# A looser hand-written order for the expert stages of a one-core decoder step

## The chip, the cores and the metric

The program runs on one core of one Trainium2 chip. The metric is the device time of one launch in microseconds (us). A core has five engines, each with its own instruction queue, worked off in order: TensorE (PE in the profile: matmuls; PEld: its weight loads), VectorE (DVE), ScalarE (ACT), GpSimd (POOL) and SyncE (SP). An instruction at the head of a queue that waits for another engine holds up everything behind it.

## The reference, cut to what matters

One layer is computed for 320 tokens (256 of a prompt, 64 of 8 decoding sequences) of width 2048: attention and a gated unit, then a layer of single-neuron experts (PEER), then a gated per-layer embedding. The change touches only the experts and what borders on them:

```python
s1 = einsum('thc,nc->thn', q[:, :, 0], k1)   # 8 heads, 128 keys
s2 = einsum('thc,nc->thn', q[:, :, 1], k2)
v1, i1 = top_k(s1, 16); v2, i2 = top_k(s2, 16)
sc, ci = top_k(v1[..., :, None] + v2[..., None, :], 16)
e = i1[ci // 16] * 128 + i2[ci % 16]         # 16 of 16384 experts per head
g = softmax(sc)
act = gelu(einsum('thkd,td->thk', u_tab[e], x))
out = einsum('thkd,thk->td', v_tab[e], g * act)
```

## The kernel before, in words

Everything is computed in fp32 accuracy with three matmuls: weights and inputs are split into a high and a low part. ACT writes the high part (`w_hi`), DVE the low part (`w_lo`), both from the weights as loaded (`w_raw`).

For 240 of the 320 tokens the experts are not gathered but computed densely: all 16384 expert rows are multiplied, and the gates of experts that were not chosen are zero. The work comes in 256 **units** of 1 MB of weights: 128 u-units (`u_tab`; 128 experts for 240 tokens, into PSUM tag "mm") and 128 v-units (`v_tab`, into tag "o"). A unit is 48 matmuls of 240 columns, a **half unit** 24. `order` lists them: 32 u-units (LEAD), then 16 **groups** of 8 v-units, with 6 or 7 u-units after each. Each PSUM tag has two buffers. The other 80 tokens (the samples and the first 16 of the prompt) are served by gathered rows: 160 row steps on DVE, spread over the groups.

Inside `manual_schedule` the order on PE, ACT and DVE is the order of the code. The functions are:

- `prepare(n, h)`: the load, `w_hi` (ACT) and `w_lo` (DVE) of half h of unit n, written two units ahead. `multiply(n, h, q)`: 12 matmuls of it (a quarter of the unit). `finish(n)`: the GELU of a u-unit (ACT, into `act`), or the addition of a v-unit to `hT` (DVE).
- Routing: `choose` picks the 16 best keys (DVE), `soften` does the softmax, `key_tables` transposes the picks on PE. A budget sets how many steps stand in each half unit: 1.5 of a cost noted at each `yield`.
- Gate map: 30 **jobs**. `one_hots(j)` makes two tables on DVE (`e`, `p`; two buffers each), `map_products(j)` 16 matmuls on PE and two copies on ACT (`g_st`, two buffers); every second job POOL writes a megabyte to `gd` in DRAM. The jobs are spread evenly over the u-units from the end of the routing to unit U1 = 29.
- `fetch_g(g)`: a transfer issued from ACT's queue that brings the gates of group g back. The first one waits for the last write to `gd`.
- `rows_of`: 16 copies on ACT (`xd`) and 16 transposes on PE, each right behind its copy, for `xc` (in units 29 to 31) and for `xx` (in group 0).
- `weights(g)`: for each of a group's 8 activations a multiplication by the gates (DVE), the high part (ACT) and the low part (DVE). One is taken per half unit, the high part in the same half unit as its multiplication. Those of group 0 stand in one block before group 0.
- `add_samples`: 32 + 16 small matmuls and three additions, all after the second v-unit of the last group.

Half of a group's eight pairs of buffers (`tails`) are columns of the tiles `a` and `c` that the dense part doesn't use; the others are four pairs of tiles `wh`, `wl`. After the groups come `emb` (the embedding product), the split of `hT` into `a` and `c`, a sum of squares, and 16 units of the last gate. That part is in the order of the scheduler.

Of the kernel before, what the change touches and what calls it, by code (L numbers as in the profile page):

```python
# [52 lines left out]
def _build(ctx, tc, nc, a):  # L53
# [554 lines left out]
    def soften(i):  # L608

        g = R[i][:, 2]  # L610
        H = g.shape[1]
        shape = [P, H, TOPK]
        z = rt.tile([P, PH], F32, name="z", bufs=3)[:, :H]
        vec.tensor_copy(z, g[:, :, 0])
        vec.tensor_sub(g, g, z.unsqueeze(2).to_broadcast(shape))
        act.activation(g, g, AF.Exp)
        yield 0.4
        vec.tensor_reduce(z, g, axis=AX.X, op=ALU.add)
        vec.reciprocal(z, z)
        vec.tensor_mul(g, g, z.unsqueeze(2).to_broadcast(shape))  # L620
        yield 0.6
# [87 lines left out]
    def rest_of_routing():  # L709
        for c in heads[6:]:  # L710
            yield from c
        softs = [soften(i) for i in range(3)]
        for _ in range(2):
            for c in softs:
                yield next(c)

# [78 lines left out]
    def rows_of(dst, tmp, sl, n):  # L795

        for c4 in range(4):
            tp = psum("tr", 512)
            for c in range(4 * c4, 4 * c4 + 4):
                xd = tmp().rearrange("p (a b) -> p a b", a=n)  # L800
                act.activation(
                    xd, hT[:, c, sl].unsqueeze(1).to_broadcast([P, n, P // n]), AF.Copy, scale=g_ffn[:, c : c + 1]
                )
                pe.transpose(tp[:, c % 4 * P : c % 4 * P + P], xd.rearrange("p a b -> p (a b)"), ident)
                if c % 2:
                    yield
            act.activation(dst[:, c4 * 512 : c4 * 512 + 512], tp, AF.Copy)
# [34 lines left out]
    def weights(g, gt):  # L842

        groups.setdefault(g, [])
        last = None
        for i in range(GRP + 1):
            if last:
                vec.tensor_sub(last[0][1], last[1], last[0][0].bitcast(F32))  # L848
                groups[g].append(last[0])
            if i < GRP:  # L850
                t = acts.pop(g * GRP + i)
                u = t.rearrange("p (a b) -> p a b", a=NTB)
                vec.tensor_mul(u, u, gt[:, :, i])
                w = tails[i] if i < 4 else [flat4(vp.tile([P, TD], F32R, name=n, bufs=GRP // 2)) for n in ("wh", "wl")]
                act.activation(w[0], flat4(t), AF.Copy)  # L855
                last = w, flat4(t)
            elif g + 1 < NG:
                state["g"] = fetch_g(g + 1)
            yield

    def add_samples():
        for c4 in range(2):
            pt = psum("tr", 512)
            for c in range(8):
                dt = 8 * c4 + c
                pe.matmul(pt[:, c * TS : c * TS + TS], xc[:, dt * P : dt * P + P], stack, start=True, stop=True)
            vec.tensor_add(
                hT[:, 8 * c4 : 8 * c4 + 8, TP:], hT[:, 8 * c4 : 8 * c4 + 8, TP:],
                pt.rearrange("p (c t) -> p c t", c=8),
            )  # L870
        pt = psum("tr", NC_ * XT)
        for c in range(NC_):
            pe.matmul(pt[:, c * XT : c * XT + XT], xx[:, c * P : c * P + P], stack_x, start=True, stop=True)  # L873
        vec.tensor_add(hT[:, :, 0:XT], hT[:, :, 0:XT], pt.rearrange("p (c t) -> p c t", c=NC_))

    state = {}
    U1 = LEAD - 3
    with tc.manual_schedule(engines={mybir.EngineType.DVE, mybir.EngineType.Activation, mybir.EngineType.PE}):
# [3 lines left out]
        routing = rest_of_routing()  # L882
        n, spent, slots = 0, 0.0, 0

        while routing:
            for h in range(2):
# [5 lines left out]
                while routing and spent < 1.5 * slots:  # L892
                    cost = next(routing, None)
                    if cost is None:
                        routing = None
                        picks = key_tables()
# [4 lines left out]
        shut(c_rt)  # L901
        c_xc, xcp = open_pool("xc")
        xc = xcp.tile([P, D], F32, name="xc")
        xx = xcp.tile([P, D], F32, name="xx")
        open_tables(picks)
        one_hots(0)
# [18 lines left out]
        tmp = lambda: vp.tile([P, P], F32, tag="xd", name="xd", bufs=1)  # L925
# [4 lines left out]
        to_c = rows_of(xc, tmp, slice(TP, T), 2)  # L930
        to_x = rows_of(xx, tmp, slice(0, XT), PH)
# [12 lines left out]

        END = len(order) - 7
# [3 lines left out]
        state["g"] = fetch_g(0)  # L949
        load = None  # L950
        m, spent, slots = 0, 0.0, 0
        for n in range(n, len(order)):
# [5 lines left out]
            if order[n][0] == "u" and order[n - 1][0] == "v":  # L958
                coming = order[n - 1][1] + 1
                groups[coming] = []  # L960
                load = weights(coming, state["g"])
            for h in range(2):
# [4 lines left out]
                if n < LEAD:  # L967
                    next(to_c, None)
                    next(to_c, None)
                    if n == LEAD - 1 and h:  # L970
                        for _ in weights(0, state["g"]):
                            pass
                elif n < LEAD + 8:
                    next(to_x, None)
                if load and (len(groups[coming]) == GRP - 1 or coming * GRP + len(groups[coming]) + 1 in acts):
                    if next(load, 0) is None:
                        spent += 0.8
                if n == LEAD and h == 0:
# [172 lines left out]
```

## Time and profile before

| what | value |
|---|---|
| median of 3 runs | 2218.16 us (2216.82 to 2222.55) |
| the profiled execution, its own time | 2219.77 us |
| its span, first to last instruction | 2218.0 us |
| mean granted TensorE clock | 0.983 |
| PE / DVE / ACT / POOL busy | 96% / 77% / 45% / 14% |

So 1.8 us of the profiled execution lie outside the span, and it is 1.6 us above the median. In a row of the timeline stand the start, the duration, the engine (a q behind it: its queue), the line and the operation; in brackets the idle time ahead of it and what ended that. In a row of windows stand the stretch, its length, and for each engine its busy time and, as (x...), its instructions; then the granted clock of TensorE, the share of the DMA engines and GB/s. A matmul counts as busy for longer than the distance to the next one, so that "busy" hides small losses; the number of matmuls in a stretch is the better measure.

### The profile page before, as it was taken

The page shows a single profiled execution, that of the slowest core. Times are in us where ns is not written, and L with a number is a line of the kernel's source. Part 1 is how long each engine was busy: PE and PEld are TensorE (multiplying, and loading weights), DVE is VectorE, ACT ScalarE, POOL GpSimd, SP SyncE. Part 2 cuts the span into 40 slices and gives each one's busy share as a digit, 9 for nine tenths or more (in the row PEclk, how much of TensorE's full clock was granted, in tenths as well). Part 3 has the DMA queues.
Part 4 walks back from the last instruction along what each step waited for, and adds up shares of the span by engine and source line. Part 5 has one row for each costly group of instructions (what it writes and reads, how often), then busy time and mean ns, then how long its engine had stood idle before and what let it go on. Part 6 is the DMA issues. An engine that isn't in the chain of part 4 may idle for free. (4 is left out here: it accounts for less than half of the span.)

```text
span 2218.0 us, 41052 instructions
## 1 busy us (share of the span) xinstructions
PE 2132.0 (96%) x17106; PEld 2070.5 (93%) x17106; DVE 1714.7 (77%) x2570; ACT 998.5 (45%) x1465; POOL 316.6 (14%) x230
## 2 busy tenths in 40 slices
PE   8999999999989889999999999999999999999899
PEld 7879999999979779999999999999999999999899
DVE  6674875899988547987887888788798888887654
ACT  5256444335457544444344444344444434443632
POOL 2000000000011101221222222121132131121000
PEclk9999999999999979999999999999999999999999
DMA  7322444334457747988988988898898898895452
GB/s 285 125 76 81 147 173 169 124 126 153 172 171 228 257 151 287 367 328 303 390 327 308 370 346 308 331 366 314 331 389 322 316 367 328 325 368 217 145 176 88
DMA packets 85209, 563.06 MB, mean 254 GB/s; under 512 B 9894, under 2 KB 14438, under 8 KB 22160
## 3 DMA queue, kind: packets, MB, share of 16 engines
q1 hardware_dynamic: 49936, 349.76, 42.6%
q0 software_dynamic: 29536, 190.83, 22.6%
q10 hardware_dynamic: 5552, 19.86, 2.5%
q8 instruction: 134, 2.20, 0.4%
q14 instruction: 51, 0.42, 0.1%
HBM read 541.58 MB, written 19.79 MB: 253 GB/s over the span
## 5 line engine op out<-in xcount | busy, mean ns | idle before, releaser
L680 DVE TENSOR_TENSOR w_lo<-w_raw,w_hi 128x1024 fp32r<-128x1024 f32 x512 | 621.0, 1221 | 276.5 <-ACT w_hi L679 275.8
L679 ACT ACTIVATE w_hi<-w_raw 128x1024 fp32r<-128x1024 f32 x512 | 537.9, 1056 | 492.4 <-PE ps_o L99 319.0
L98 PE MATMUL ps_mm<-a,w_hi 128*128 128x240 f32 (+1 forms) x1776 | 522.0, 294 | 26.5 <-ACT act L702 24.3
L99 PE MATMUL ps_mm<-a,w_hi 128*128 128x240 f32 (+1 forms) x1776 | 520.3, 293 | 1.0 <-DVE a L123 1.0
L100 PE MATMUL ps_mm<-a,w_lo 128*128 128x240 f32 (+1 forms) x1776 | 517.7, 292 | 2.1 <-DVE w_lo L680 1.6
L98 PEld LDWEIGHTS ps_mm<-a,w_hi 128*128 128x128 f32 x1776 | 338.2, 190 | 37.7 <-ACT act L702 29.1
L100 PE MATMUL ps_mm<-c,w_lo 128*128 128x240 f32 (+1 forms) x1280 | 362.9, 284 | 2.0 <-DVE w_lo L680 2.0
L98 PE MATMUL ps_mm<-c,w_hi 128*128 128x240 f32 (+1 forms) x1280 | 364.4, 285 | 0.0
L99 PE MATMUL ps_mm<-c,w_hi 128*128 128x240 f32 (+1 forms) x1280 | 362.8, 283 | 0.0
L99 PEld LDWEIGHTS ps_mm<-a,w_hi 128*128 128x128 f32 x1776 | 338.1, 190 | 9.0 <-issue 6.6
L100 PEld LDWEIGHTS ps_mm<-a,w_lo 128*128 128x128 f32 x1776 | 338.0, 190 | 6.4 <-issue 3.2
L99 PE MATMUL ps_o<-wl,w_hi 128*128 128x240 f32 x1024 | 284.2, 278 | 4.1 <-DVE wl L848 4.1
L81 ACT ACTIVATE w_hi<-w_raw 128x1024 fp32r<-128x1024 f32 x150 | 158.7, 1060 | 283.1 <-PE ps_mm L99 188.9
L100 PE MATMUL ps_o<-wh,w_lo 128*128 128x240 f32 x1024 | 284.1, 277 | 0.0
L98 PE MATMUL ps_o<-wh,w_hi 128*128 128x240 f32 x1024 | 281.4, 275 | 0.3 <-ACT wh L855 0.3
L82 DVE TENSOR_TENSOR w_lo<-w_raw,w_hi 128x1024 fp32r<-128x1024 f32 x150 | 182.7, 1221 | 92.3 <-ACT w_hi L81 88.7
L100 PEld LDWEIGHTS ps_mm<-c,w_lo 128*128 128x128 f32 x1280 | 245.2, 192 | 2.2 <-DVE w_lo L680 2.1
L98 PEld LDWEIGHTS ps_mm<-c,w_hi 128*128 128x128 f32 x1280 | 245.6, 192 | 0.0
L99 PEld LDWEIGHTS ps_mm<-c,w_hi 128*128 128x128 f32 x1280 | 245.2, 192 | 0.0
L99 PEld LDWEIGHTS ps_o<-wl,w_hi 128*128 128x128 f32 x1024 | 194.3, 190 | 5.2 <-DVE wl L848 5.2
L98 PEld LDWEIGHTS ps_o<-wh,w_hi 128*128 128x128 f32 x1024 | 196.1, 192 | 1.5 <-ACT wh L855 1.5
L100 PEld LDWEIGHTS ps_o<-wh,w_lo 128*128 128x128 f32 x1024 | 196.0, 191 | 0.0
(366 smaller groups left out, 3815.4 us busy)
## 6 DMA issues: line engine op xcount, KB each, us to landing
w_raw<-in_uT SPq DMA_DIRECT2D x128, 1024.0 KB, 6.9
w_raw<-in_v_t SPq DMA_DIRECT2D x128, 1024.0 KB, 7.8
w_raw<-in_w_in SPq DMA_DIRECT2D x25, 1024.0 KB, 5.0
w_raw<-in_w_out SPq DMA_DIRECT2D x16, 1024.0 KB, 4.8
w_raw<-in_wq SPq DMA_DIRECT2D x16, 1024.0 KB, 4.7
w_raw<-in_w_gate SPq DMA_DIRECT2D x16, 1024.0 KB, 5.0
gd<-g_st POOLq DMA_DIRECT2D x15, 1024.0 KB, 6.8
g_t<-gd ACTq DMA_DIRECT2D x16, 960.0 KB, 4.7
```

Source lines behind the costliest of these rows:

```text
L81: last = act.activation(hi, s, AF.Copy)
L82: (lo_eng or vec).tensor_sub(lo, s, hi.bitcast(F32))
L98: pe.matmul(out, wh, xh, start=start, stop=False)
L99: pe.matmul(out, wh, xl, start=False, stop=False)
L100: pe.matmul(out, wl, xh, start=False, stop=stop)
L679: act.activation(hi, s, AF.Copy)
L680: vec.tensor_sub(lo, s, hi.bitcast(F32))
```

## The change

Eight edits, all inside the hand-written order or in what feeds it:

1. `soften` runs as seven small steps for all three tables together; `key_tables`, `open_tables` and the first `one_hots` become steps of the same budget, which is 1.4 a half unit where it was 1.5.
2. The routing so ends after unit 22 (before: after unit 17), and U1 is 28. The 30 jobs stand in units 23 to 27, three in each half unit; before they stood in units 18 to 28, behind a first quarter.
3. `rows_of`: each transpose stands one step after its copy, and a step is a quarter of a unit for `xc` (units 28 to 31) and a half unit for `xx` (group 0). `xd` has two buffers where it had one.
4. `weights`: multiplication, high part and low part of one activation stand in three successive half units.
5. `weights(0)` is spread over the last three half units before group 0.
6. The last group uses eight buffers of `act` in place of the columns of `a` and `c`.
7. `add_samples` is cut in two: the samples are added when their row steps are done, the first 16 tokens in the last group.
8. The budget of the row steps counts eight steps per group, where it counted up to nine.

```diff
-    def soften(i):
-        g = R[i][:, 2]
...
+    def soften():
+        gs = [R[i][:, 2] for i in range(3)]
...
+        for g, z in zip(gs, zs):
+            vec.tensor_copy(z, g[:, :, 0])
+            vec.tensor_sub(g, g, wide(z))
+            yield 0.5
+        for g in gs:
+            act.activation(g, g, AF.Exp)
+        yield 1.4
...
     def rows_of(dst, tmp, sl, n):
+        xd = None
+        for c in range(NC_ + 1):
+            if xd is not None:
+                if c % 4 == 1:
+                    tp = psum("tr", 512)
+                pe.transpose(tp[:, (c - 1) % 4 * P : (c - 1) % 4 * P + P], xd, ident)
+            if c < NC_:
+                xd = tmp()
...
     def weights(g, gt):
-        for i in range(GRP + 1):
-            if last:
-                vec.tensor_sub(last[0][1], last[1], last[0][0].bitcast(F32))
...
+        for i in range(GRP + 2):
+            if i >= 2:
+                vec.tensor_sub(w[i - 2][1], flat4(u[i - 2]), w[i - 2][0].bitcast(F32))
+                groups[g].append(w[i - 2])
             if i < GRP:
...
+                vec.tensor_mul(m, m, gt[:, :, i])
+            elif i == GRP and g + 1 < NG:
                 state["g"] = fetch_g(g + 1)
+            if 1 <= i <= GRP:
+                k = i - 1
+                if k < 4 and g < NG - 1:
+                    w[k] = tails[k]
+                elif k < 4:
+                    w[k] = [flat4(up.tile([P, TD], F32R, tag="act", name=n, bufs=LEAD)) for n in ("th", "tl")]
...
+                act.activation(w[k][0], flat4(u[k]), AF.Copy)
             yield
...
-    U1 = LEAD - 3
+    U1 = LEAD - 4
...
+    def front():
+        for c in heads[6:]:
+            yield from c
+        yield from soften()
+        picks = key_tables()
+        yield 2.0
...
+        open_tables(picks)
+        yield 2.8
+        one_hots(0)
+        yield 2.8
...
-                while routing and spent < 1.5 * slots:
+                while steps and spent < 1.4 * slots:
...
+        state["g"] = fetch_g(0)
+        to_c = rows_of(xc, state["xd"], slice(TP, T), 2)
+        to_x = rows_of(xx, state["xd"], slice(0, XT), PH)
+        load = weights(0, state["g"])
+        for n in range(n, LEAD):
+            finish(n - 1)
+            for h in range(2):
+                for q in range(2):
+                    multiply(n, h, q)
+                    next(to_c, None)
+                if 2 * (n - U1) + h >= 5:
+                    for _ in range(3):
+                        next(load, None)
...
-            if order[n] == ("v", NG - 1, 1):
-                add_samples()
```

What this does to the queues is shown at three places. **First, the gate map.** ACT's queue there, before (`g_st` are the copies of a job's products, `w_hi` the high part of a coming half unit, `act` a GELU):

```order
L679 ACTIVATE w_hi<-w_raw 128x1024
L702 ACTIVATE act<-ps_mm 128x240
L783 ACTIVATE g_st<-ps_o 128x4x128 x2
L783 ACTIVATE g_st<-ps_s 128x4x128 x2
L679 ACTIVATE w_hi<-w_raw 128x1024
L783 ACTIVATE g_st<-ps_o 128x4x128 x2
L679 ACTIVATE w_hi<-w_raw 128x1024
```

A `w_hi` follows the copies of one or two jobs. The same queue and place after the change:

```order
L683 ACTIVATE w_hi<-w_raw 128x1024
L779 ACTIVATE g_st<-ps_o 128x4x128 x2
L779 ACTIVATE g_st<-ps_s 128x4x128 x2
L779 ACTIVATE g_st<-ps_o 128x4x128 x2
L683 ACTIVATE w_hi<-w_raw 128x1024
L706 ACTIVATE act<-ps_mm 128x240
```

Now it follows the copies of three. On DVE, in the same place after the change, the low part stands behind the tables of three jobs, and ahead of those of the next three:

```order
L684 TENSOR_TENSOR w_lo<-w_raw,w_hi 128x1024
L762 TENSOR_TENSOR e<-i_6912,sel_6914 128x2048
L763 TENSOR_TENSOR p<-e,sel_6914 128x2048
L762 TENSOR_TENSOR e<-i_6912,sel_6914 128x2048
L763 TENSOR_TENSOR p<-e,sel_6914 128x2048
L762 TENSOR_TENSOR e<-i_6912,sel_6914 128x2048
L763 TENSOR_TENSOR p<-e,sel_6914 128x2048
L684 TENSOR_TENSOR w_lo<-w_raw,w_hi 128x1024
```

Before, one or two such pairs stood between two `w_lo`. **Second, the u-units between two groups**, DVE's queue before (`act<-act,g_t` multiplies by the gates, `a_78<-act,a_78` makes the low part of the weights):

```order
L853 TENSOR_TENSOR act<-act,g_t 128x240
L680 TENSOR_TENSOR w_lo<-w_raw,w_hi 128x1024
L848 TENSOR_TENSOR a_78<-act,a_78 128x4x60
L853 TENSOR_TENSOR act<-act,g_t 128x240
L680 TENSOR_TENSOR w_lo<-w_raw,w_hi 128x1024
```

The same place after the change:

```order
L854 TENSOR_TENSOR act<-act,g_t 128x240
L684 TENSOR_TENSOR w_lo<-w_raw,w_hi 128x1024
L854 TENSOR_TENSOR act<-act,g_t 128x240
L684 TENSOR_TENSOR w_lo<-w_raw,w_hi 128x1024
L849 TENSOR_TENSOR a_78<-act,a_78 128x4x60
L854 TENSOR_TENSOR act<-act,g_t 128x240
```

The first low part has moved one half unit down; ACT's copy stands between, one half unit behind its multiplication. **Third, the transposes of `xc` on PE**, before (between them stand 24 matmuls):

```order
L100 MATMUL ps_mm<-a_78,w_lo 128x240
L804 MATMUL ps_tr<-ident,xd 128x128 x4
L98 MATMUL ps_mm<-c,w_hi 128x240
L99 MATMUL ps_mm<-c,w_hi 128x240
L100 MATMUL ps_mm<-c,w_lo 128x240
```

After the change one transpose stands there, and 12 matmuls lie between two of them. The first still comes after 24 matmuls of the first unit behind the gate map:

```order
L100 MATMUL ps_mm<-a_78,w_lo 128x240
L798 MATMUL ps_tr<-ident,xd 128x128
L98 MATMUL ps_mm<-c,w_hi 128x240
L99 MATMUL ps_mm<-c,w_hi 128x240
L100 MATMUL ps_mm<-c,w_lo 128x240
```

More of the change, by code (lines that the diff above doesn't have):

```diff
@@ L707, in finish @@
         del sums[n], halves[n]
[L709 to L715, printed above, removed]
     NB = 8
@@ L881, in _build @@
                 prepare(n, h)
-        routing = rest_of_routing()
+        steps = front()
         n, spent, slots = 0, 0.0, 0
-        while routing:
+        while steps:
             for h in range(2):
@@ L942, in row @@
                 rows[m] = k.fetch(j, second)
+        state["g"] = fetch_g(0)
[11 more added lines that the diff above has]
+                        next(load, None)
+                if n == LEAD - 1 and h == 0:
+                    for m in range(3):
+                        row(m)
+                prepare(n + 2, h)
+        for _ in to_c:
+            pass
         END = len(order) - 7
@@ L948, in _build @@
         total = sum(extra(n) for n in range(LEAD, END)) + 0.8 * GRP * NG + step_us * len(steps)
-        state["g"] = fetch_g(0)
-        load = None
         m, spent, slots = 0, 0.0, 0
-        for n in range(n, len(order)):
+        sums_c = add_samples()
+        sums_x = None
+        for n in range(LEAD, len(order)):
             finish(n - 1)
@@ L966, in _build @@
                     spent += extra(n)
[L967 to L975, printed above, removed]
-                    if next(load, 0) is None:
-                        spent += 0.8
-                if n == LEAD and h == 0:
-                    for k in range(3):
-                        row(k)
-                if n >= LEAD:
-                    slots += 1
-                    while m < len(steps) and (spent + step_us / 2 < total * slots / (2 * (END - LEAD)) or n >= END):
-                        k, j, second = steps[m]
-                        k.step(j, second, rows.pop(m))
-                        row(m + 3)
-                        m += 1
-                        spent += step_us
+                next(to_x, None)
+                if load and (at_ >= GRP or coming * GRP + at_ in acts):
+                    if next(load, 0) is None:
+                        at_ += 1
+                        spent += 0.8 if at_ <= GRP else 0.0
+                if m >= len(steps) - 16:
+                    next(sums_c, None)
+                if sums_x:
+                    next(sums_x, None)
+                slots += 1
+                while m < len(steps) and (spent + step_us / 2 < total * slots / (2 * (END - LEAD)) or n >= END):
+                    k, j, second = steps[m]
+                    k.step(j, second, rows.pop(m))
+                    row(m + 3)
+                    m += 1
+                    spent += step_us
+                if m == len(steps) and not sums_x and n >= END:
+                    sums_x = add_first()
                 if n + 2 < len(order):
                     prepare(n + 2, h)
-            if order[n] == ("v", NG - 1, 1):
-                add_samples()
         finish(n)
```

72 lines of the change are left out of this document (30 added, 42 removed).

## Prediction, made before the changed kernel ran

> **What bounds the kernel now.** The page gives the shares, the windows view cuts the span at the borders of the stages, and the view of waits tells who held PE up. The page's row:
>
> ```profile
> PE 2132.0 (96%) x17106; PEld 2070.5 (93%) x17106; DVE 1714.7 (77%) x2570; ACT 998.5 (45%) x1465; POOL 316.6 (14%) x230
> ```
>
> PE bounds the kernel, and the change leaves its work as it is. So only what PE loses counts. The stages, in order: A the routing, B the key tables, C the gate map, D the last u-units before group 0, E group 0, F everything up to group 15, G group 15, H the start of the embedding stage. The ninth row is one plain v-group without a wait:
>
> ```profile
> 522.94:622.55 99.61, 96.01 (x837) 95.39 (x837) 95.06 (x301) 41.42 (x52) 0.00 (x0) 0.98 0.49 170
> 622.55:638.57 16.02, 7.45 (x44) 6.88 (x43) 12.10 (x32) 7.69 (x16) 4.04 (x8) 0.79 0.53 173
> 638.57:757.34 118.77, 116.78 (x996) 113.91 (x996) 93.84 (x79) 81.14 (x90) 16.23 (x14) 0.99 0.70 217
> 757.34:799.43 42.09, 28.85 (x164) 25.72 (x161) 7.69 (x8) 16.25 (x32) 4.24 (x4) 0.76 0.53 198
> 799.43:860.07 60.64, 55.34 (x400) 50.17 (x401) 42.29 (x51) 26.61 (x44) 10.90 (x6) 0.89 0.63 230
> 860.07:2015.54 1155.47, 1127.58 (x9987) 1122.01 (x9985) 961.11 (x990) 495.68 (x630) 252.91 (x150) 1.00 0.87 338
> 2015.54:2076.13 60.59, 55.82 (x450) 55.14 (x449) 43.83 (x51) 26.40 (x39) 4.07 (x2) 0.92 0.52 185
> 2076.13:2101.41 25.28, 19.47 (x110) 18.46 (x109) 17.35 (x28) 18.05 (x36) 0.00 (x0) 0.86 0.29 103
> 894.86:937.85 42.99, 42.99 (x386) 42.99 (x385) 39.84 (x40) 17.24 (x17) 12.47 (x8) 1.00 0.94 375
> ```
>
> A group is 384 matmuls by the code: 42.99 / 384 = 0.112 us each, 5.37 a unit. The products of one job take 757.34 - 755.53 = 1.81 us, and the wait that follows the gate map stands in the same timeline of PE:
>
> ```profile
> 755.53 2.05 PE L779 MATMUL ps_o<-p,e 128*128 128x128 f16 x16
> 757.34 0.36 PE L98 MATMUL ps_mm<-a,w_hi 128*128 128x240 f32 x1
> 767.23 0.48 PE L804 MATMUL ps_tr<-ident,xd 128*128 128x128 f32 x1 [6.96 <-ACT xd L801]
> ```
>
> With the counts of the code the stages lose: A 99.61 - 836 x 0.112 = 6.0; B 16.02 - 36 x 0.112 = 12.0; C 118.77 - 516 x 0.112 - 30 x 1.81 = 6.7; D 42.09 - 3 units = 26.0; E 60.64 - 43.0 = 17.6; F 1155.47 - 208 units = 38; G 60.59 - 43.0 = 17.6, with the additions' small matmuls; H 25.28 - 106 matmuls of 320 columns at 0.149 = 9. Some 133 us, of which only the additions are work. The longest waits of PE, and those matmuls:
>
> ```profile
> PE ps_mm L98 <- ACT act L702: 24.3, 25, 2.3
> PE ps_tr L804 <- ACT xd L801: 17.2, 22, 7.0
> PE ps_s L779 <- DVE p L767: 5.4, 3, 4.2
> PE ps_tr L728 <- DVE r L620: 4.4, 1, 4.4
> ```
>
> ```profile
> 2031.79 3.68 PE L866 MATMUL ps_tr<-c_stack,xc 128*128 128x64 f32 x32
> ```
>
> The second half of the additions has 32 instructions as well, so 7.4 us of G stay. The four rows of waits make 51 us, well under half. Much of the rest is a slower clock behind a wait. Behind a wait of 1.95 us matmuls are spaced 0.21 instead of 0.11 us for a while, and the six us around it were granted 0.72; behind one of 1.65 us that isn't seen:
>
> ```profile
> 586.57 0.38 PE L100 MATMUL ps_mm<-c,w_lo 128*128 128x240 f32 x1 [1.95 <-DVE w_lo L680]
> 586.00:592.00 6.00, 5.43 (x34) 5.43 (x35) 5.72 (x22) 1.32 (x2) 0.00 (x0) 0.72 0.51 176
> 612.00:620.00 8.00, 6.35 (x55) 5.92 (x53) 7.70 (x23) 2.60 (x3) 0.00 (x0) 1.00 0.44 152
> 614.23 0.38 PE L100 MATMUL ps_mm<-a,w_lo 128*128 128x240 f32 x1 [1.65 <-DVE w_lo L680]
> ```
>
> So a wait over some 2 us costs 6 x 0.28 = 1.7 us more (my estimate from these rows), a shorter one nothing.
>
> **The change part by part.** *F, the groups.* One activation, on ACT, DVE and PE:
>
> ```profile
> 877.07 2.29 DVE L828 SCALAR_TENSOR_TENSOR row<-row,xc 128x2048 f32<-128x2048 f32 x1
> 880.74 0.40 DVE L853 TENSOR_TENSOR act<-act,g_t 128x240 f32<-128x240 f32 x1
> 881.18 0.41 ACT L855 ACTIVATE wh<-act 128x240 fp32r<-128x240 f32 x1 [2.63 <-DVE act L853]
> 882.43 0.35 ACT L702 ACTIVATE act<-ps_mm 128x240 f32<-128x240 f32 x1
> 882.84 0.38 PE L98 MATMUL ps_mm<-a,w_hi 128*128 128x240 f32 x1 [1.16 <-ACT act L702]
> ```
>
> DVE multiplies only after a row step of 2.29 us and a `w_lo`; ACT's copy waits 2.63 us for it; behind the copy stand the `w_hi` and the GELU that frees PE's buffer; PE waits 1.16. With the copy one half unit (2.7 us) behind its multiplication, ACT finds it done unless DVE is later than that. Two row steps in a row make DVE about two half units late by these durations, and the GELU then still has most of a unit before PE asks for its buffer. So these waits go. I leave 4 of the 38 us, for waits that row transfers cause: minus 34. The extra wait of the low part costs nothing: it has one more half unit too.
>
> *D.* ACT's transfer of the gates still waits for the last write to `gd`, and the copies `xd` stand behind it:
>
> ```profile
> 759.09 1.15 POOL L790 DMA_DIRECT2D gd<-g_st  x1 [6.89 <-ACT g_st L783]
> 766.14 0.33 ACTq L839 DMA_DIRECT2D g_t<-gd  x1
> ```
>
> The third order place of the change section shows 24 matmuls ahead of the first transpose, as before, so that this wait stays: 7.2 us, and 2.7 for the clock behind it (twice 1.7 at most). What goes are the waits behind single copies (the row of `xd` above: 17.2 us in 22 waits, so 0.49 each without the longest; 13 of them in D) and the slow clock that they prolonged. A transpose alone between matmuls I price at 0.28 us:
>
> ```profile
> 826.76 0.27 PE L804 MATMUL ps_tr<-ident,xd 128*128 128x128 f32 x1
> 824.00:838.00 14.00, 12.42 (x104) 11.56 (x104) 9.96 (x11) 7.03 (x14) 3.90 (x2) 1.00 0.65 244
> ```
>
> 16 x 0.28 = 4.5, so D loses 14.4 where it lost 26.0: minus 11.6. *E*: the block of `weights(0)` is gone from its head, and `xx` has its transposes a half unit behind their copies: 4.5, and 1.2 for the last low part, which stands behind a `w_lo`, in place of 17.6: minus 11.9.
>
> *B.* Both waits (4.4 for the softmax, 4.2 for the first `p`) had no work in between; now each step stands two or three half units ahead of its reader. 1.0 remains for six transposes: minus 11.0. *A*: with 1.4 for 1.5 DVE has 7% less routing in each half unit, in more of them. The two waits of A came some 23 and 32 half units into it (586.57 and 614.23, from 522.94), so the backlog grows slowly, and what was saved can be spent again in the added ones; I take half of the 6.0 away, between none and all: minus 3.0.
>
> *G*: no burst of row steps, no flush that waits (the last group needs unit 127's GELU, 0.35, a multiplication and a copy of 0.4 each, within the 21 x 0.112 = 2.35 us until PE wants its eighth activation), additions moved earlier. 17.6 less the 7.4 of work, and 0.3 for what stays: minus 9.9. *H*: the 16 splits of `hT` stood together on ACT ahead of the first copy of `emb`, because they overwrite the columns that group 15 read:
>
> ```profile
> 2074.50 3.72 ACT L118 ACTIVATE a<-hT,c_gains 128x320 fp32r<-128x320 f32 x8
> 2083.86 0.63 PE L98 MATMUL ps_s<-p_h,w_hi 128*128 128x320 f32 x1 [5.81 <-ACT emb L1011]
> ```
>
> They now run during group 15. But the squares and the split of `p_t` come later than before, and PE waits for `p_h`: about 2.5, and 2.5 for the clock and for `emb`. Minus 4.0, between minus 9 and plus 1.
>
> *C, the gate map, is what the change pays.* The one wait that PE had there shows a loop through four engines:
>
> ```profile
> 727.27 2.06 PE L779 MATMUL ps_s<-p,e 128*128 128x128 f16 x16
> 730.28 1.06 ACT L679 ACTIVATE w_hi<-w_raw 128x1024 fp32r<-128x1024 f32 x1
> 731.37 1.23 DVE L680 TENSOR_TENSOR w_lo<-w_raw,w_hi 128x1024 fp32r<-128x1024 f32 x1 [1.02 <-ACT w_hi L679]
> 732.51 1.22 DVE L766 TENSOR_TENSOR e<-i,sel 128x2048 f16<-128x2048 f16 x1
> 734.91 1.22 DVE L766 TENSOR_TENSOR e<-i,sel 128x2048 f16<-128x2048 f16 x1
> 735.05 0.64 PE L779 MATMUL ps_s<-p,e 128*128 128x128 f16 x4 [1.14 <-DVE p L767]
> ```
>
> Products, then their copies, behind these the `w_hi`, then the `w_lo`, behind it the next tables, then products: 735.05 - 727.27 = 7.78 us, 5.97 after the end of the first products. Before, PE had more matmuls to fill this; now there are three jobs (5.43) and 24 matmuls (2.7) in each half unit, 8.1 in all, and DVE itself needs three pairs of tables (734.91 - 732.51 = 2.4 each) and a `w_lo` (732.51 - 731.37 = 1.14): 8.3. The loop closes once in each half unit, since `w_hi` stands behind three jobs' copies. The half units alternate: two jobs behind the first 12 matmuls and one behind the others, then one and two. With one-two, the second job starts 5.97 after the end of the last half unit, the third a pair of tables later (2.4), and ends 1.81 on: 10.2. With two-one: 5.97, job 1.81, 12 matmuls 1.4, job 1.81: 11.0. In the first half unit the second job waits for `w_hi`, `w_lo` and one pair of tables (1.06, 1.14, 2.5 with the way to PE), then 1.81, 1.4, 1.81: 9.9. Sum: 9.9 + 5 x 10.2 + 4 x 11.0 = 104.9, with a wait of 2.7 us in four of them (1.7 each for the clock: 6.8). Work: 5 x 5.37 + 54.3 = 81.2. C loses 30.5 where it lost 6.7: **plus 23.8**. Bounds of the loss: 6.7 (PE hides it as before) and 39 (the clock falls in all nine). POOL's queue keeps its order; a write to `gd` takes 7 us from issue to landing (759.09 to 766.14), and two jobs make 111.7 / 15 = 7.4, so that two buffers of `g_st` still do; were they short, ACT's copies would wait, and the loop with them.
>
> [...]
>
> Sum: -34 - 11.6 - 11.9 - 11.0 - 3.0 - 9.9 - 4.0 + 23.8 = -61.6. The profiled execution took 2219.77, so the changed one 2158; that execution is 1.6 above the median of 2218.16, so a median of 2156.6.
>
> **The rivals.** *1, C is hidden*: PE hides the loop as before. For it: PE's work (81.2) and DVE's (10 x 8.3) are nearly level. Against it: the wait above. 23.8 less: 2133. *2, F keeps its waits*: ACT is held by DVE a half unit later as well. For it: DVE is busy 961 of 1155 us in F. Against it: two half units of slack. 34 more: 2191. *3, the clock stays low in D and E*, because transposes stand in so many places: as in the slowest ten us of D:
>
> ```profile
> 770.00:780.00 10.00, 8.38 (x42) 7.73 (x43) 2.32 (x2) 4.98 (x11) 0.00 (x0) 0.67 0.74 311
> ```
>
> 12 units at 0.67 are 64.4 x 0.49 = 32 more: 2188. Against it: the granted 1.00 at 824 to 838, with two transposes in every 24 matmuls. [...]
>
> *4, slower than before*: the loop in C closes with every job, not every third. Then 30 x 7.78 = 233 us against 112 in my sum (104.9 + 6.8): 121 more, 2278. It turns the sign where C takes over 173 us, that is from about 4.5 closings in six jobs on. For it: a `w_lo` waited for its `w_hi` (1.02 above) already before. Against it: the order has one `w_hi` for three jobs.
>
> *That the change doesn't do what it says* is excluded for the order (the rows show it), and for its effect it is rival 2.
>
> **How the numbers follow.** The forecast 0.70; rival 1 0.12, rival 2 0.08, rival 3 0.05, rival 4 0.05. The forecast's own range is 2142 to 2173 (C 6 to 9 either way, A 3, D 3, F 5, H 5, not all one way). To leave out no more than 2 in 10 it takes in most of rivals 1 and 3 and half of rival 2: 2130 to 2190. A measurement can tell about 0.3%, 6.6 us, from no change. All but rival 4 lie beyond it: faster 0.95. Of rival 4, 0.02 are closings that just cancel the gain: same 0.02, slower 0.03.
>
> **What would show it.** Right: PE's waits for the GELU in F (24.3 us) near zero; no wait at the key transposes; one wait of about 7 us at the first `xd`; in C, PE waiting for `p` once or twice in each half unit, 1 to 3 us each, the stage 100 to 120 us long, with a clock under 0.95; a wait for `p_h` or `p_l` where 5.81 stood. Wrong: F's waits for the GELU over 10 us; C under 90 us (rival 1) or over 130; a granted clock below 0.8 in the v-units of group 0.

## The result, and the profile after

The changed kernel takes 2155.14 us (median of 4 runs, 2153.34 to 2158.39), the kernel before, run beside it, 2220.36 (2216.82 to 2222.9): a ratio of 0.9709, 95% interval 0.9689 to 0.9729. The forecast was 2156.6. The profiled execution took 2153.34 us with a span of 2151.5, so 66.4 us less than the profiled one of before; the steps of the forecast add up to 61.6.

The page's first row of the kernel after has the same 17106 matmuls on PE:

```profile
PE 2103.3 (98%) x17106; PEld 2053.0 (95%) x17106; DVE 1718.2 (80%) x2570; ACT 1004.5 (47%) x1465; POOL 323.8 (15%) x230
```

The windows of the kernel after, cut at the same borders: A the routing, B the key tables, C the gate map (here with its first 12 matmuls), D the last u-units before group 0, E group 0, F the groups up to 15, G group 15, H the start of the embedding stage:

```profile
522.52:632.67 110.15, 108.04 (x957) 107.39 (x957) 105.16 (x321) 51.58 (x66) 0.00 (x0) 1.00 0.51 182
632.67:649.41 16.74, 16.74 (x153) 16.74 (x151) 12.64 (x20) 8.15 (x15) 4.04 (x8) 1.00 0.67 227
649.41:760.87 111.46, 93.00 (x723) 88.17 (x721) 80.74 (x68) 68.45 (x74) 16.22 (x14) 0.86 0.60 183
760.87:793.00 32.13, 25.08 (x212) 24.73 (x209) 12.55 (x18) 19.06 (x39) 4.25 (x4) 0.89 0.77 288
793.00:843.46 50.46, 48.31 (x400) 47.92 (x401) 38.83 (x43) 24.66 (x40) 10.07 (x6) 0.93 0.75 279
843.46:1964.35 1120.89, 1120.61 (x10020) 1120.42 (x10019) 976.47 (x997) 503.53 (x632) 264.47 (x151) 1.00 0.91 351
1964.35:2016.29 51.94, 47.62 (x418) 46.91 (x416) 35.06 (x49) 28.25 (x42) 0.59 (x1) 1.00 0.49 178
2016.29:2034.67 18.38, 18.15 (x106) 16.96 (x107) 14.44 (x21) 15.48 (x32) 0.00 (x0) 0.91 0.33 115
```

Work is counted as in the prediction: a matmul 0.112 us, a unit 5.37, a group 43.0, a job 1.81, a matmul of 320 columns 0.149. C, for instance, has 240 x 0.112 + 30 x 1.81 = 81.2 us of work, and loses 111.46 - 81.2 = 30.3. The wait for `p_h` at the border of G and H (3.5 us) is counted to H, where its forerunner of before stood; G then loses 51.94 - 43.0 - 3.5 = 5.4, H 18.38 - 106 x 0.149 + 3.5 = 6.1 (before, with the decimal that the prediction rounded off, 25.28 - 106 x 0.149 = 9.5). The stages against the forecast, in us:

| stage | lost before | lost after | change | forecast |
|---|---|---|---|---|
| A | 6.0 | 3.1 | -2.9 | -3.0 |
| B | 12.0 | 0.6 | -11.4 | -11.0 |
| C | 6.7 | 30.3 | +23.6 | +23.8 |
| D | 26.0 | 10.6 | -15.4 | -11.6 |
| E | 17.6 | 7.5 | -10.1 | -11.9 |
| F | 38 | 3.4 | -34.6 | -34 |
| G | 17.6 | 5.4 | -12.2 | -9.9 |
| H | 9.5 | 6.1 | -3.4 | -4.0 |

The changes add up to 66.4. PE's longest waits from A to H in the kernel after (us in total, times, longest):

```profile
PE ps_o L775 <- DVE p L763: 10.6, 10, 2.4
PE ps_s L775 <- DVE p L763: 7.8, 5, 3.5
PE ps_tr L798 <- ACT xd L801: 7.0, 1, 7.0
PE ps_s L98 <- ACT p_h L118: 3.5, 1, 3.5
PE ps_o L99 <- DVE wl L849: 3.2, 3, 2.1
```

The 24.3 us for the GELU are gone. At the top stand 15 waits for `p`, 18.4 us, all in C, where the prediction found one. Counted from start to start in PE's timeline they cost 21.7 us, since the view counts the last matmul as busy for a while after PE has nothing to do (the 16 products at 690.53 are shown as 2.06 us, and the next matmul starts 1.81 us after them). Of the remaining 8.6 of C's 30.3 us, somewhat under 2 go to the change between two kinds of matmul, and the rest, some 7, to a slower clock (0.86 granted, against 0.99 before).

One turn of the loop in C, in the timeline of PE, ACT and DVE. Products, then `w_hi`, `w_lo`, tables, products:

```profile
693.48 1.07 ACT L683 ACTIVATE w_hi<-w_raw 128x1024 fp32r<-128x1024 f32 x1
693.77 2.06 PE L775 MATMUL ps_s<-p,e 128*128 128x128 f16 x16
694.58 1.23 DVE L684 TENSOR_TENSOR w_lo<-w_raw,w_hi 128x1024 fp32r<-128x1024 f32 x1 [1.71 <-ACT w_hi L683]
695.72 1.22 DVE L762 TENSOR_TENSOR e<-i,sel 128x2048 f16<-128x2048 f16 x1
696.98 1.23 DVE L763 TENSOR_TENSOR p<-e,sel 128x2048 f16<-128x2048 f16 x1
698.26 2.05 PE L775 MATMUL ps_o<-p,e 128*128 128x128 f16 x16 [2.43 <-DVE p L763]
```

DVE stands idle for 1.71 us because `w_hi` comes late, and only behind the `w_lo` does it make the tables that PE then waits 2.43 us for.

### The profile page after: what moved, and what is told of

The parts are those of the page before. It is cut to its first block, busy times and chain, and to the rows that moved or that the text cites. A ratio compares the mean times of both kernels' runs of the same rounds, so it can differ in the third digit from the quotient of the medians.

```text
span 2151.5 us, 41052 instructions
## 1 busy us (share of the span) xinstructions
PE 2103.3 (98%) x17106; PEld 2053.0 (95%) x17106; DVE 1718.2 (80%) x2570; ACT 1004.5 (47%) x1465; POOL 323.8 (15%) x230
## 5 line engine op out<-in xcount | busy, mean ns | idle before, releaser
L98 PEld LDWEIGHTS ps_mm<-c,w_hi 128*128 128x128 f32 x1280 | 242.8, 190 | 0.0
L99 PEld LDWEIGHTS ps_mm<-c,w_hi 128*128 128x128 f32 x1280 | 242.5, 189 | 0.0
```

What stands on the lines that cost most here:

```text
L98: pe.matmul(out, wh, xh, start=start, stop=False)
L99: pe.matmul(out, wh, xl, start=False, stop=False)
```

## The experiments

The durations of stages below come from windows cut as above, in the kernel named.

**1. The loop.** If the loop is what C pays, it opens when the tables of one more job stand ahead of the low part. Nothing else moves:

```diff
         first, job = n, 0
+        one_hots(1)
...
-                        if job + 1 < JOBS:
-                            one_hots(job + 1)
                         map_products(job)
                         job += 1
+                        if job + 1 < JOBS:
+                            one_hots(job + 1)
```

> The changed kernel, with each job's two tables made one job earlier (behind the products of the job before last instead of ahead of the products of the last one), so that on DVE one pair of tables that stood behind a low part of the weights now stands ahead of it. The same instructions, the same buffers. Loop theory (products, copies, high part, low part, tables, products): the first two jobs of every half unit have their tables before the low part is waited for, the loop is open, and C takes 82 to 92 us instead of 111.6, bounded by DVE's own work (10 half units of 8.3 us); the time falls by 20 to 28 us from 2155, to about 2131. Rival, the write-back: 15 writes of the gate map one behind the other at about 7 us each from issue to landing make 105 us whatever the tables do: C stays over 104 us and the time over 2148. Rival, too much work in one place: PE and DVE are so nearly level in work that neither order helps: C falls by less than 8 us.

Measured: 2135.77 us (2135.17 to 2137.46), ratio to the kernel before 0.9615 (0.9597 to 0.9633). The window of C:

```profile
651.58:743.38 91.80, 86.90 (x723) 84.00 (x721) 80.58 (x68) 67.16 (x74) 16.22 (x14) 0.94 0.69 217
```

The waits of the same kernel: PE's for `p` (before the edit 15 waits, 18.4 us), ACT's for a write of the gate map ahead of a copy, and ACT's at the transfer of the gates, behind C:

```profile
PE ps_o L775 <- DVE p L763: 4.5, 2, 3.1
ACT g_st L779 <- DMA gd<-g_st: 12.5, 7, 5.4
ACT act L706 <- DMA gd<-g_st: 7.7, 1, 7.7
```

C fell from 111.5 to 91.8 us by the order of DVE alone, with the same work: the loop theory holds, and the theories of the write-back (C over 104 us) and of too much work in one place fall. Part of what is left of C's loss (91.8 - 81.2 = 10.6) is a wait that the loop had hidden: ACT now waits seven times for a write of the gate map.

**2. A third buffer for the copies `g_st`.** Every third one lies in the tile of `xx`, which is free until group 0:

```diff
-            oh["st"] = oh["pool"].tile([P, NK, 16], F32, name="g_st")
+            if tb % 3 == 2:
+                oh["st"] = state["rows"][1].rearrange("p (a t) -> p a t", t=16)
+            else:
+                oh["st"] = oh["pool"].tile([P, NK, 16], F32, name="g_st")
```

> The changed kernel, with a third buffer for the copies of the products (every third one lies in the tile of xx, which is not used before group 0). Loop theory: ACT waited for a write to the gate map once, 4.7 us, and only that wait goes: C 107 to 110 us instead of 111.6, the time 2 to 5 us lower, 2150 to 2153. Rival, the write-back bounds C: C falls below 100 us and the time below 2144.

Measured: 2158.62 us (2157.08 to 2161.69), ratio 0.9723 (0.9704 to 0.9743): no gain over the changed kernel. C and D:

```profile
649.95:759.04 109.09, 93.34 (x723) 88.44 (x721) 80.71 (x68) 69.02 (x74) 16.22 (x14) 0.87 0.61 187
759.04:796.32 37.28, 27.57 (x212) 27.22 (x209) 12.55 (x18) 19.11 (x39) 4.26 (x4) 0.83 0.65 245
```

PE's wait at the first transpose:

```profile
PE ps_tr L801 <- ACT xd L804: 9.7, 1, 9.7
```

C fell by 2.4 us as expected, so that the write-back did not bound it. The time did not fall: D rose by 5.2, since the transfer of the gates waits for the last write all the same, and the wait of 7.0 us became 9.7. The last write itself landed later, as POOL's timeline shows:

```profile
760.18 1.05 POOL L822 DMA_INDIRECT row<-in_u_rows,c_e  x1 [5.09 <-PE ps_o L778]
761.21 1.23 POOL L789 DMA_DIRECT2D gd<-xx  x1
```

It is issued 1.4 us earlier than in the changed kernel (761.21 for 762.62), but behind a fetch of rows, with two more right behind it. In the changed kernel the first fetch stands behind that write (764.08), and the next one waits 5.20 us for it to land (770.46). The transfer of the gates could go 10.6 us after the issue here (771.78), and 7.1 us after it there (769.76). I had counted a gain in one stage without asking what the next one waits for.

**3. Edit 4 undone in the changed kernel.** The high part stands beside its multiplication again:

```diff
-        for i in range(GRP + 2):
-            if i >= 2:
+        for i in range(GRP + 1):
+            if i >= 1:
...
-            if 1 <= i <= GRP:
-                k = i - 1
+            if i < GRP:
+                k = i
```

> The changed kernel with its fourth edit alone undone: the high part of an activation stands in the same half unit as its multiplication, as before the change. Forecast's theory (ACT's copy waits for DVE's multiplication, and the GELU behind it holds PE's buffer): PE's waits for the GELU come back, over 20 us in F, and F takes 25 to 38 us longer: 2180 to 2193, about 2189. Rival, F was mended by the other edits (the budget of the row steps, the buffers of the last group): PE's waits for the GELU stay under 8 us and the time within 10 us of 2155.

Measured: 2205.01 us (2199.84 to 2205.43), ratio 0.992 (0.9898 to 0.9942). F:

```profile
845.20:2015.46 1170.26, 1132.52 (x10020) 1125.08 (x10019) 971.66 (x998) 496.44 (x633) 261.51 (x151) 1.00 0.87 336
```

PE's longest waits in F:

```profile
PE ps_mm L98 <- ACT act L706: 25.3, 26, 1.7
PE ps_o L98 <- DVE hT L710: 7.8, 9, 1.7
```

The waits for the GELU are back; the direction and the mechanism hold. But F is 49 us longer, not 25 to 38, and nine waits for the additions to `hT` stand beside them. The next two runs are for that surplus.

**4. Edit 4 alone, on the kernel before**, its budget of row steps kept:

```diff
-                    if next(load, 0) is None:
-                        spent += 0.8
+                    if next(load, 0) is None:
+                        at_ += 1
+                        spent += 0.8 if at_ <= GRP + 1 else 0.0
```

with `weights` as after the change, and `tails` for every group.

> The kernel before with the fourth edit alone: multiplication, high part and low part of an activation in three successive half units, the budget counting as before. Forecast's theory: PE's waits for the GELU in F (24.3 us) go and F takes 1119 to 1128 us instead of 1155.5, the other stages stay: 2218 - 34 = 2184 (2180 to 2193). Rival, with the row steps as before DVE itself is late and the waits go to the additions to hT or to the low parts: F stays over 1140.

Measured: 2172.02 us (2171.09 to 2176.47), ratio 0.9783 (0.9767 to 0.9799), some 47 us less than the kernel before beside it (2219.28) where I expected 34; it lies below the expected interval. F:

```profile
858.49:1975.46 1116.97, 1116.83 (x9986) 1116.64 (x9985) 967.23 (x992) 503.17 (x631) 249.85 (x150) 1.00 0.92 351
```

F lost all of its 38 us (1155.5 to 1117.0), where the forecast had left 4; E lost 5.0 less (55.6 for 60.6) and G 2.3 less. PE has no wait in F at all.

**5. Edits 4 and 8 undone in the changed kernel**, that is, experiment 3 with the budget counting nine steps:

```diff
-                        spent += 0.8 if at_ <= GRP else 0.0
+                        spent += 0.8
```

> As the kernel of the third experiment (the changed kernel, high part at once), with the eighth edit undone too: the budget of the row steps counts nine steps per group again. There F took 49 us more, where the forecast's term was 34, and nine waits for the additions to hT (7.8 us) stood beside those for the GELU. Theory: the eighth edit puts more row steps in F and the surplus of 15 is theirs: F 1150 to 1160 instead of 1170, some 5 to 10 us of it come back in G as a burst of row steps; 2190 to 2202. Rival, the surplus has another cause: F over 1165.

Measured: 2203.11 us (2202.83 to 2210.56), ratio 0.9935 (0.9913 to 0.9957). F and G:

```profile
843.23:2004.75 1161.52, 1131.29 (x10020) 1125.70 (x10019) 963.01 (x994) 496.76 (x632) 254.66 (x150) 1.00 0.87 337
2004.75:2065.19 60.44, 52.47 (x419) 51.48 (x417) 44.46 (x53) 29.04 (x43) 4.05 (x2) 0.91 0.51 189
```

F is 8.7 us shorter than in experiment 3 and G 8.5 longer (51.97 there). F missed its interval by 1.5 us, and the total by one. So the eighth edit shifts row steps from G into F, a zero sum as long as ACT waits for DVE. With edit 4 in place they cost next to nothing in F: the kernel after loses 3.4 us there, about what the additions that were moved into F take. That G then keeps the gain is likely but not shown, since no run undoes the eighth edit alone.

**6. The squeeze alone, on the kernel before.** The jobs wait until unit 24:

```diff
+        while n < U1 - 5:
+            for h in range(2):
+                for q in range(2):
+                    multiply(n, h, q)
+                    if h == 0 and q == 0:
+                        finish(n - 1)
+                prepare(n + 2, h)
+            n += 1
         first, job = n, 0
```

> The kernel before, with nothing changed but the place of the 30 jobs: they wait until unit 24 and stand in units 24 to 28, three in each half unit, as the change has them in 23 to 27. Forecast's theory (the loop closes in each half unit once there is too little other work to fill it): units 18 to 23 run without a wait and units 24 to 28 take about 111 us, 24 more in all than the 118.8 of before: 2242 (2236 to 2248), and PE waits for p over ten times. Rival, the loss in C came from the other edits: less than 8 us more.

Measured: 2237.28 us (2233.83 to 2243.71), ratio 1.0073 (1.0056 to 1.009): slower than before by some 16 us by the ratio, and inside the expected interval. The windows of units 18 to 23 without jobs (with the half unit ahead of them), and of the jobs:

```profile
631.43:667.98 36.55, 36.55 (x314) 36.55 (x314) 21.25 (x28) 17.47 (x27) 4.04 (x8) 0.95 0.55 191
667.98:778.17 110.19, 93.22 (x722) 88.35 (x721) 80.72 (x68) 68.69 (x74) 16.23 (x14) 0.87 0.61 185
```

The five units with three jobs in each half unit take 110 us here too, at a granted 0.87 (0.86 in the changed kernel). The price of C is the squeeze and no other edit. (Part of it comes back at once: the wait of 4.2 us for the first `p` is gone, since its tables now have six units' time.)

**7. The transfer of the gates later**, behind the copies for the first five transposes:

```diff
-        state["g"] = fetch_g(0)
         to_c = rows_of(xc, state["xd"], slice(TP, T), 2)
...
-        load = weights(0, state["g"])
...
+                if at_ == 2:
+                    load = weights(0, fetch_g(0))
```

> The changed kernel, with ACT's transfer of the first gates placed three half units later, behind the copies for the first five transposes. Theory (the transfer stands at the head of ACT's queue and waits for the last write to the gate map, the copies behind it): PE's wait of 7.0 us at the first transpose goes and with it 2 to 3 us of slow clock; D takes 22 to 25 us instead of 32.1; the time falls by 7 to 10 us, to about 2146. Rival, the transfer is then too late for the multiplications by the gates in the last three half units: what D gains group 0 loses again, and the time stays within 3 us of 2155.

Measured: 2149.53 us (2146.29 to 2151.43), ratio 0.9673 (0.9653 to 0.9693), so 5.6 us less than the changed kernel; D:

```profile
762.77:789.78 27.01, 25.90 (x212) 25.37 (x209) 12.63 (x18) 19.06 (x39) 4.71 (x4) 0.92 0.88 337
```

The first multiplications by the gates, in DVE's timeline:

```profile
783.03 0.72 DVE L854 TENSOR_TENSOR act<-act,g_t 128x240 f32<-128x240 f32 x2 [1.43 <-DMA g_t<-gd]
```

The wait of 7.0 us is gone (1.1 us are left there), D is 5.1 shorter, less than expected, and group 0 is as before (50.4). The last row shows why there is little more to be had: DVE already waits for the gates.

**8. Edit 3 undone**: one buffer of `xd`, each transpose right behind its copy.

```diff
-            if xd is not None:
...
-                pe.transpose(tp[:, (c - 1) % 4 * P : (c - 1) % 4 * P + P], xd, ident)
...
+                pe.transpose(tp[:, c % 4 * P : c % 4 * P + P], xd, ident)
+                if c % 2:
+                    yield
```

> The changed kernel with its third edit alone undone: one buffer of xd, each transpose right behind its copy, two or four of them together after a half unit. Forecast's theory (PE waits about half a microsecond for each copy): some 30 waits come back at 0.5 each, 7 us in D and 8 in group 0, the longest wait (7 us, for the gates) stays: the time rises by 10 to 18 us, to 2165 to 2173. Rival, the waits for single copies were a consequence of the block that the fifth edit took away: the time stays within 4 us of 2155. Rival, transposes in many places hold the clock down: the time falls.

Measured: 2175.75 us (2174.47 to 2177.2), ratio 0.9799 (0.9783 to 0.9816), 20.6 more than the changed kernel, somewhat over the expected interval. PE's waits for `xd`:

```profile
PE ps_tr L801 <- ACT xd L797: 16.3, 21, 6.5
```

D and E:

```profile
763.29:810.29 47.00, 34.60 (x212) 31.71 (x210) 11.86 (x17) 19.52 (x39) 4.25 (x4) 0.77 0.51 187
810.29:867.18 56.89, 50.38 (x402) 47.54 (x401) 40.11 (x43) 25.11 (x41) 10.17 (x6) 0.94 0.70 257
```

D has its loss of before again (47.0 - 21.5 = 25.5, where it was 26.0), E takes 6.4 more. The twenty short waits make 9.8 us, 0.49 each, the number that the forecast had used; beside them stands a slower clock, granted 0.77 in D. Counted from start to start in PE's timeline, D and E take 21.3 us more than in the changed kernel; by my estimate from these distances some 14 of them are waits and some 5 the slower clock. The rival of transposes that hold the clock down falls, and so does the one that laid the waits to the block of `weights(0)`.

**9. Tables ahead and a third buffer together** (the edits of 1 and 2).

> Tables one job ahead and a third buffer for the copies together. With the loop open, ACT waited seven times for a write to the gate map, 12.5 us in all. Theory: C falls from 91.8 to 83 to 87 us, the work of PE (81) and DVE (83) in it; but the last write, and with it the transfer of the gates that holds up the first transposes, comes no earlier by the same amount, so that D gives back 3 to 6 us, as it did with the third buffer alone: 2131 to 2138 in all, where the tables alone made 2135.8. Rival, the gain in C stays: 2128 or less.

Measured: 2134.54 us (2132.11 to 2136.2), ratio 0.9615 (0.9599 to 0.9631). C and D:

```profile
650.43:737.97 87.54, 85.57 (x722) 82.56 (x721) 80.38 (x68) 68.34 (x74) 16.22 (x14) 0.98 0.72 227
737.97:774.13 36.16, 25.08 (x211) 24.73 (x209) 12.55 (x18) 19.13 (x39) 4.25 (x4) 0.86 0.73 269
```

What ACT waits for behind the last `w_hi` of C, in its timeline:

```profile
751.27 0.37 ACT L706 ACTIVATE act<-ps_mm 128x240 f32<-128x240 f32 x1 [11.02 <-DMA gd<-xx]
```

C is 4.3 us shorter than with the tables alone, at a clock of 0.98, just over the expected 83 to 87 us. The total is the same within the runs' spread: the wait for the last write has grown to 11 us. ACT could issue the transfer at 750.9 here and at 752.9 with the tables alone, though C ended 5.4 us earlier here.

**10. All three, and `p_t` loaded early** (1, 2, 7, and `p_t` in a buffer of the weights, loaded by SP).

```diff
-        p_t = pl.tile([P, 2, T], F32, name="p_t", bufs=1)
-        pool.dma_start(p_t, a["pT"])
+        p_t = raw.tile([P, 16, P], F32, name="w_raw").rearrange("p a b -> p (a b)")[:, : 2 * T]
+        p_t = p_t.rearrange("p (c t) -> p c t", c=2)
+        nc.sync.dma_start(p_t, a["pT"])
```

> Tables one job ahead, a third buffer, the transfer of the gates three half units later, and the input p_t of the embedding loaded by SP into a buffer of the weights (its own buffer becomes free only with the last matmul of group 15, and PE then waited 3.5 us). Theory: the gains add up, since each takes away the wait that ends last in its own stage: C 83 to 87 us instead of 111.6, D 25 to 28 instead of 32.1, H 3 to 6 less, E as it is: 2155 - 26 - 5 - 4 = 2120 (2115 to 2126). Rival, the way from the last write over the transfer of the gates to the multiplications of group 0 is the real bound: group 0 loses 5 to 12 us more at its start, 2126 to 2133.

Measured: 2127.41 us (2127.0 to 2127.98), ratio 0.9584 (0.9568 to 0.96): faster than both kernels, and the best of the study, but 7 short of the middle of the theory and in the rival's interval. D:

```profile
738.57:769.23 30.66, 26.61 (x212) 25.94 (x209) 12.64 (x18) 18.78 (x39) 4.42 (x4) 0.89 0.83 318
```

In the timeline, ACT's wait for the last write, and the start of the embedding on ACT and PE:

```profile
752.70 1.06 ACT L683 ACTIVATE w_hi<-w_raw 128x1024 fp32r<-128x1024 f32 x1 [5.65 <-DMA gd<-xx]
1986.85 3.45 ACT L142 ACTIVATE sq<-hT 128x320 f32<-128x320 f32 x6 [1.08 <-DVE ssq L143]
1991.98 0.64 PE L98 MATMUL ps_s<-p_h,w_hi 128*128 128x320 f32 x1 [3.63 <-ACT emb L1052]
```

C took 87.8 us, as in 9. Two things ate the rest. The transfer, three half units later, still waits for the last write (5.65 us), which is done at 751 to 753 in all three kernels so far with the tables ahead (1, 9 and this one). Group 0 lost nothing more (47.5 us), so that the place of the loss is D and not the one that the rival named. And the early `p_t` brought nothing: the wait of 3.5 for `p_h` is gone and one of 3.6 for `emb` stands there, because six squares of `hT` stand ahead of `emb` in ACT's queue. G is 3.6 shorter (48.3), what follows 4.0 longer.

**11. The same, with the budget of the routing back at 1.5 and U1 = 27.**

```diff
-    U1 = LEAD - 4
+    U1 = LEAD - 5
...
-                while steps and spent < 1.4 * slots:
+                while steps and spent < 1.5 * slots:
```

and the steps of `weights(0)` in the last four half units.

> As the kernel before, and in addition the budget of the routing back at 1.5 and the end of the gate map one unit earlier (27), so that the jobs lie in six units and group 0 has one unit more to get its gates and weights, whose steps stand in the last four half units. Theory: A loses 2 to 3 us more with the tighter routing, C loses less than 5 us against its work of 86.5, and the 5.5 us that group 0 loses at its start go: 2115 (2110 to 2120). Rival, the tighter routing costs more than that: A and B lose over 8 us more, the time is not under that of the kernel before.

Measured: 2130.01 us (2126.61 to 2133.44), ratio 0.959 (0.9574 to 0.9606), not under experiment 10. The window of A:

```profile
526.82:636.50 109.68, 103.51 (x885) 102.53 (x885) 102.92 (x320) 48.11 (x63) 0.00 (x0) 0.97 0.49 173
```

PE's waits in it:

```profile
PE ps_mm L100 <- DVE w_lo L684: 3.7, 2, 2.0
PE ps_mm L98 <- ACT act L706: 2.5, 1, 2.5
```

With 884 matmuls A loses 109.68 - 99.0 = 10.7 us, against 3.1 to 4.7 at the budget of 1.4. C lost 2.8 us (89.3 against a work of 86.5) and group 0 only 2.2 (45.15), both as theory had it. But A's 6 to 8 us, and a D that lost 0.9 us more, took that back, and the time is the rival's.

## Why the prediction was right, point by point

- **C, +23.8 forecast, +23.6 measured.** The mechanism is shown: it goes with the order of the tables (1) and comes with the squeeze alone (6). The forecast's times for a half unit fit too. Of the five put at 10.2 us four took 10.1 (the one from 682.23 to 692.34, for instance) and one 12.5; the four put at 11.0, or 12.7 with the clock, took 11.7 to 12.1; the first took 10.7 where it was 9.9. Two details were off and cancelled, which is luck. The waits, from start to start, cost 21.7 us and not 23.7, and about 2 us go to the change between products and matmuls, which the forecast had left out (12 matmuls between two jobs take 1.43 us and not 1.34, twenty times; experiment 10 paid that as well). And "two buffers of `g_st` still do" failed once: ACT waited 4.7 us for a write, and PE then 3.46.
- **"Waits over some 2 us slow the clock, a shorter one costs nothing"** is the step that does not hold. In C the granted clock was 0.50 behind a wait of 1.27 us (rows in the last section), and the length of a wait alone does not tell it. The forecast had put the clock of C at 6.8 us by four waits of 2.7 us; it comes out about right (some 7), by more and shorter ones.
- **F, -34 forecast, -34.6 measured.** Edit 4 takes the GELU waits away, as shown from both sides (3, 4). The step "I leave 4 of the 38" failed in kind: of PE's waits 0.3 us are left. The 3.4 us lost in F are the first half of the additions, which edit 7 moved from G: work, as the prediction says, but counted there in G. That -34 and -34.6 agree so closely is luck.
- **D, -11.6 forecast, -15.4 measured.** The wait for the gates stayed (7.0 for 7.2), and the waits for single copies went; undoing edit 3 brought them back (8). The term that was mis-sized is the transpose, 0.28 us each: 12 matmuls and a transpose take 1.45 us here, against 1.34 for the 12 alone, so 0.11 each, 2.7 us less for 16. The rest is the clock, put at 2.7 us: the 12 matmuls and the transpose behind the long wait took 2.82 us at a granted 0.50 (770.85 to 773.67), so 1.4 more than the 1.45; the next 12 and their transpose took 1.54, and those behind them 1.45.
- **E, -11.9 forecast, -10.1 measured.** "1.2 for the last low part" was too small: the first unit of group 0 took 10.91 us for 5.37 of work, with a wait of 2.1 for `wl` and, behind it, matmuls 0.21 us apart to the end of the unit (a granted clock of 0.72 over its eleven us). So that term was some 5.5 us; what hid most of the miss is the term of 4.5 for the 16 transposes of `xx`, which at 0.11 each make 1.8. Experiment 11, with the low parts earlier, got the loss of that unit down to half a microsecond.
- **A and B** came as forecast. For A, the half that was taken away is a matter of the budget: at 1.5 the changed steps lose 10.7 us (11).
- **G and H** together: -15.6 measured, -13.9 forecast. The wait for `p_h` stands where forecast (3.5 for 2.5). That ACT's queue would bring `emb` late too is what experiment 10 uncovered.
- **The sum** was made for the profiled execution, and there it was 4.8 us short (61.6 for 66.4), mostly D. That the median lies only 1.5 us from the forecast is in part luck: the profiled execution was the fastest of its four runs, where that of before was above its median.

Of the rivals, C hidden by PE's other work did not happen (111.5 us), though by order most of it could have been had (87.5 in experiment 9). F's waits did not stay. The clock did not stay low in D and E: from 804.00 to 843.46, with a transpose behind every 24 matmuls, the granted clock was 0.99. The loop did not close with every job, which would have made C 233 us long.

One thing stays open: what delays the last write of the gate map. With two buffers of `g_st` the transfer of the gates could go 7.1 us (changed kernel) and 7.8 us (experiment 1) after the issue of that write; with three it went 10.6, 10.8, 11.5 and 12.8 us after it (2, 9, 10 and 11). In these four POOL issues one fetch of rows right ahead of the write and two right behind it, so that the fetches are the likely cause; no run moves them away from the write.

## What to carry to other kernels

Where several engines hand work round in fixed orders, look for the loop (here products, copies, high part, low part, tables), count how often it closes, and move one producer ahead of the link that waits: some 20 us came from moving two lines and making the first tables one job earlier, with the same instructions. Price a gain through to the next stage: a third buffer and an earlier load both did what they should, and gave it back to the wait that stood behind them. An instruction that waits for another engine belongs one step behind its producer, above all when something that frees a buffer is queued behind it (here some 47 us in experiment 4 and 20.6 us in experiment 8).

## What the runs showed of the hardware that was not expected

**These products kept their pace at a granted clock of 0.50.** Windows of the kernel after around three jobs of 16 products each, and behind the last of them 12 matmuls of 240 columns (the granted clock is the third number from the end):

```profile
705.73:707.55 1.82, 1.82 (x19) 1.79 (x17) 0.00 (x0) 1.47 (x2) 0.00 (x0) 1.00 0.81 243
712.60:714.40 1.80, 1.80 (x16) 1.78 (x16) 1.76 (x2) 0.59 (x1) 0.00 (x0) 0.50 0.76 216
722.71:724.52 1.81, 1.81 (x16) 1.81 (x17) 1.78 (x2) 0.66 (x1) 0.00 (x0) 0.50 1.02 206
724.52:726.30 1.78, 1.78 (x12) 1.78 (x10) 1.75 (x3) 1.36 (x2) 0.01 (x1) 0.57 1.00 387
```

At a granted 1.00 and at 0.50 the 16 products take the same 1.80 to 1.82 us, 0.113 each, so a lost clock cost these products nothing. What sets their pace is not shown. The matmuls of 240 columns behind the last of them were slower: from 724.87 to 725.93, at a granted 0.50, their starts are 0.21 apart, where 0.11 is their distance at 1.00 (692.54 to 693.65).

**A clock of 0.50 behind a short wait.** The products at 722.71 came behind a wait of 1.27 us. Those ahead of the wait, from 719.39, had a granted 1.00 (from 716.00 to 719.20 it was 0.50); the windows above show 0.50 during the ones at 722.71 and 0.57 in the 12 matmuls behind. PE's timeline:

```profile
722.71 2.06 PE L775 MATMUL ps_o<-p,e 128*128 128x128 f16 x16 [1.27 <-DVE p L763]
```

The length of the waits alone does not tell the clock. Behind two waits of 1.11 and 0.35 us (ahead of the products at 666.04 and at 668.43) the granted clock was 0.50 from 668.43 to 670.23; behind two of 1.08 and 0.34 us (688.13 and 690.53) it stayed at 1.00 from 690.53 to 692.34.

In C's trace 15 waits for `p` of up to 3.5 us stand close together, and the granted clock changes between 0.50 and 1.00. What decides it is not shown.

**A transpose alone among matmuls** costs about 0.11 us: the starts of three in a row, 12 matmuls between them, are 1.45 us apart, where 12 matmuls alone take 1.34.

```profile
775.21 0.27 PE L798 MATMUL ps_tr<-ident,xd 128*128 128x128 f32 x1
776.66 0.27 PE L798 MATMUL ps_tr<-ident,xd 128*128 128x128 f32 x1
778.11 0.27 PE L798 MATMUL ps_tr<-ident,xd 128*128 128x128 f32 x1
```
